# A three-layer float32 transformer on one core: unsplit value products in the first mixer, transposed retention queries, and another order of the first loads

## The chip, the cores and the metric

One core of a Trainium2 chip runs the whole program. The metric is the device time of one execution in microseconds (us), here the median of three. TensorE (PE) multiplies, ScalarE (ACT) and VectorE (DVE) work elementwise, GpSimd (POOL) does a few small things, SyncE (SP) issues most of the transfers.

## The reference

All is float32, one sequence of 256 tokens, width 1024. Two layers of a first block, each a mixer and a squared-ReLU MLP of width 4096, are followed by a hybrid layer with three attention branches and a final RMS norm. The change touches the two mixers:

```
def _window_gqa(q, k, v, sink):            # heads a: 8 query heads of 64, 2 key/value heads
...
    p = jnp.exp(s - m)
    p = p / (jnp.sum(p, axis=-1, keepdims=True) + jnp.exp(sk - m))
    o = jnp.einsum('bnhgqk,bnkhd->bqnhd', p.astype(v.dtype), vb)
...
def _even_mixer(x, norm_g, w_in, qn_a, kn_a, sink_a, qn_b, kn_b, rpb_b, w_out):     # first mixer
...
    qa, ka, va, qb, kb, vb = _split(h @ w_in, EVEN_SPLITS)
...
    return jnp.concatenate([oa, ob], axis=-1) @ w_out
...
def _odd_mixer(x, norm_g, w_in, dec_f, dec_b, gn_g, w_out):     # second mixer: retention, 8 heads
...
    q, k, v, g = _split(h @ w_in, ODD_SPLITS)
...
        a = jnp.einsum('bhid,bhjd->bhij', qc, kc) * dmask
        o = jnp.einsum('bhij,bhjv->bhiv', a, vc) + jnp.einsum('bhid,bhdv->bhiv', qc, R) * cross[:, :, None]
```

Heads b are neighbourhood attention, 8 heads of 64. Retention's queries and keys are 128 wide for each head, its values 256.

## The kernel before, in words

**Products.** Nearly every float32 product is made of three fast ones. A float32 operand is split into a high part (rounded to the type F32R, by ACT) and a low part (the difference, by DVE); `mm3` (L337 to L340) adds high by high, high by low and low by high. A few small products are unsplit: both operands stay F32, and PE takes the four-pass float32 path. In the rows such a product shows as two records.

**Panels.** A weight matrix comes in panels of 512 columns, 1024 rows, as two loads of 1 MB (tile `raw`, four buffers, `w_dma` L400). `w_hi` (ACT) and `w_lo` (DVE) turn each load into two pairs of tiles `whi` and `wlo`; for the MLP's input weights, once its pool is open, the pairs are called `mhi` and `mlo` and lie at another offset (`w_tile`, L440). `panel` (L495) keeps the activations stationary and moves 512 weight columns: 2 token tiles x 8 row tiles x 3 = 48 matmuls of 512 columns, result tokens by columns. `panel_T` (L542) keeps the weights stationary and moves 256 tokens: 4 x 8 x 3 = 96 matmuls of 256 columns, result columns by tokens. It serves the MLPs.

**Start.** `run` (L847) issues the first loads: the transposed input, the first panel in small pieces, then x (for the norm's statistics), constants, and the next two loads (the second panel, 256 columns wide, 512 KB each). `warm` (L883) gives PE small bf16 matmuls on zeros until the weights come. The first panel (`first_panel`, L516) makes the queries of heads a, the second their keys and values (ka, va), the third the queries of heads b (qb), then kb, vb, and two panels of another layer's memory keys and values (kx, vx).

**First mixer.** `qk_task` squares a panel's result on ACT (tile `qn`), reduces it on DVE, adds the norm's `em`, scales and transposes. The 16 heads go in pairs: `score_pair` (L723) makes both heads' scores, one on rows 0 to 63 and one on rows 64 to 127 of the array; `even_head` (L737) makes the softmax (tile `p`), four transposes on PE, splits the result into `ph` and `pl`, and multiplies by the split values (`vah`, `val`, `vbh`, `vbl`). Values are padded with zeros to 128 columns (`pads`, L992), so that two heads add into the two halves of one bank's rows, 6 matmuls of 256 columns for each.

**Second mixer.** `_odd` runs over four pairs of heads; for each pair one panel gives queries and keys (512 columns), one the values, one the gate. The query task (L1264) copies the panel's result to `nat`, and `split_T` (L673) transposes it four blocks at a time and splits it into `qkh` and `qkl`.

**Order.** The program is laid down by a planner of its own: generators yield conditions, `drive` (L157) keeps a model of when each engine, transfer and tile is free, and at each step takes the ready task with the best priority. Each engine executes its instructions in the order in which they were laid down. Constants of that model (rate of loads, start times such as `MEM`, `BIAS`, `DMA0`) move the order and nothing else.

Of the kernel before, what the change touches and what calls it, by code (L numbers as in the profile page):

```python
# [72 lines left out]
class Kernel:  # L73
# [17 lines left out]
    MEM, BIAS = 14.0, 16.0  # L91

    DMA0, FINE = 1.5, 4
# [299 lines left out]
    def load(self, eng, out, in_):  # L393

        eng.dma_start(out, in_)
        n = out.shape[0] * self._n(out) * 4
        self.free["D"] += max(n / 360e3, 0.18)
        self._mark(self.ready, out, self.free["D"] + 1.7, "D")

    def w_dma(self, a=None, b=4):  # L400
# [13 lines left out]
        else:  # L414
            self.nc.sync.dma_start(raw[:, :n], src)
            t0 = max(self.free["D"], self.rawfree[i - self.RAW] if i >= self.RAW else 0.0)
            self.free["D"] = t0 + P * n * 4 / 360e3
# [259 lines left out]
    def split_T(self, src, hi, lo, k0, t, key, scale=None):  # L677
# [8 lines left out]
        if k0 is None:  # L686
            pv = ps[:, :n * P].rearrange("p (a b q) -> p a b q", a=2, b=n // 2)
        else:
            pv = ps[:, :n * P].rearrange("p (i q) -> p i q", i=n)
            hi, lo = (v[:, k0:k0 + n, t * P:(t + 1) * P] for v in (hi, lo))  # L690
# [46 lines left out]
    def even_head(self, pool, ps, v, o, j, tab, init, sink=None):  # L737
# [25 lines left out]
        yield ("rdy", p)  # L763
        yield ("acq", "pT", 1)
        yield ("acq", "bank", 1)
# [10 lines left out]
        out = o[:, (j // 2 % 2) * S:(j // 2 % 2 + 1) * S]  # L776
        if j % 4:
            yield ("ev", ("pv", j - 1))
        yield ("op", "T", [], [ph, pl])
# [6 lines left out]
        self.fire(("pv", j), at=self.free["T"])  # L786
        self.give("pT")
        self.give("hd")
# [53 lines left out]
    def run(self):  # L842
# [24 lines left out]
        self.w_dma(0, 4)  # L867
        for t in range(NT):
            self.load(nc.sync, x[t], aps["x"][t * P:(t + 1) * P, :])
        self.load(nc.sync, const, aps["const"][:, :K_MAIN])  # L870
        for _ in range(self.RAW - 2):
            self.w_dma()
# [9 lines left out]
    def warm(self):  # L882
# [6 lines left out]
        yield 1.4  # L889
        while self.hcur < 3:  # L890
# [4 lines left out]
            self._pe(0.213 if self.now < 7 else 0.11, ps)  # L895
# [36 lines left out]
    def _even(self, pool):  # L932
# [899 lines left out]
```

## Time and profile before

| | |
|---|---|
| median of 3 runs | 996.02 us (996.0 to 997.14) |
| profiled execution, its own time | 997.11 us |
| its span, first to last instruction | 995.3 us |
| PE busy | 982.2 us, 99% of the span |
| DVE busy, ACT busy | 675.1 us (68%), 525.9 us (53%) |
| bytes read | 173.75 MB, 176 GB/s over the span |
| mean granted clock of PE | 0.997 |

The span is read from the first to the last instruction; the own time of the execution is 1.8 us longer. Busy shares are means over the whole span; what matters for an edit is which engine is waited for in its stage. Ends of matmuls are modelled, so that consecutive ones overlap in the rows: the distance between two starts is the price of one.

### The profile page before, as it was taken

The page shows a single profiled execution, that of the slowest core. Times are in us where ns is not written, and L with a number is a line of the kernel's source. Part 1 is how long each engine was busy: PE and PEld are TensorE (multiplying, and loading weights), DVE is VectorE, ACT ScalarE, POOL GpSimd, SP SyncE. Part 2 cuts the span into 40 slices and gives each one's busy share as a digit, 9 for nine tenths or more (in the row PEclk, how much of TensorE's full clock was granted, in tenths as well). Part 3 has the DMA queues.
Part 4 walks back from the last instruction along what each step waited for, and adds up shares of the span by engine and source line. Part 5 has one row for each costly group of instructions (what it writes and reads, how often), then busy time and mean ns, then how long its engine had stood idle before and what let it go on. Part 6 is the DMA issues. An engine that isn't in the chain of part 4 may idle for free.

```text
span 995.3 us, 14096 instructions
## 1 busy us (share of the span) xinstructions
PE 982.2 (99%) x5559; PEld 844.6 (85%) x5559; DVE 675.1 (68%) x1134; ACT 525.9 (53%) x821; POOL 30.4 (3%) x38
## 2 busy tenths in 40 slices
PE   8999999999999999999999999999999999999997
PEld 6787889999998888888889999998888888878885
DVE  6898567554457977877657555446779866677774
ACT  7777656433345655555446553334564554454453
POOL 1220000000000000000000000000100000000000
PEclk9999999999999999999999999999999999999999
DMA  9733455555445544443555555542544436544431
GB/s 351 285 133 122 134 175 205 218 209 202 170 169 175 184 166 163 167 168 138 194 187 171 209 209 214 212 171 97 203 157 141 156 139 205 192 173 148 180 127 42
DMA packets 27266, 175.71 MB, mean 177 GB/s; under 512 B 3200, under 2 KB 3584, under 8 KB 7616
## 3 DMA queue, kind: packets, MB, share of 16 engines
q1 hardware_dynamic: 25776, 171.49, 48.0%
q0 software_dynamic: 704, 2.49, 1.0%
q8 instruction: 43, 0.70, 0.3%
q10 hardware_dynamic: 720, 0.84, 0.3%
q14 instruction: 23, 0.19, 0.1%
HBM read 173.75 MB, written 1.05 MB: 176 GB/s over the span
## 4 chain that ended last, share of the span: by engine, by line
PE 97%; DVE 2%; ACT 0%; DMA 0%; issue 0%; POOL 0%; DVEq 0%; POOLq 0%
PE bank L332 93%; PE bank L343 4%; DVE p L279 1%; DMA tb<-in_xT 0%; DVE pl L257 0%; DVE p L265 0%; DVE st L289 0%; PE bank L894 0%; ACT ph L252 0%; ACT nraw L252 0%; ACT u L252 0%; DVE x L257 0%; DVE wlo L257 0%; ACT qn L252 0%; DVE o L257 0%
## 5 line engine op out<-in xcount | busy, mean ns | idle before, releaser
L257 DVE TENSOR_TENSOR wlo<-raw,whi 128x1024 fp32r<-128x1024 f32 (+2 forms) x266 | 311.5, 1183 | 89.6 <-ACT whi L252 87.9
L252 ACT ACTIVATE whi<-raw 128x1024 fp32r<-128x1024 f32 (+2 forms) x266 | 268.5, 1024 | 131.9 <-PE bank L332 131.3
L332 PE MATMUL bank<-whi,xh 128*128 128x512 f32 (+2 forms) x592 | 233.8, 397 | 2.2 <-ACT whi L252 2.2
L332 PE MATMUL bank<-wlo,xh 128*128 128x512 f32 (+2 forms) x592 | 227.5, 384 | 0.4 <-DVE wlo L257 0.4
L332 PE MATMUL bank<-whi,xl 128*128 128x512 f32 (+2 forms) x592 | 227.7, 385 | 0.0
L332 PEld LDWEIGHTS bank<-whi,xh 128*128 128x128 f32 x592 | 112.2, 190 | 23.0 <-ACT whi L252 3.1
L332 PEld LDWEIGHTS bank<-whi,xl 128*128 128x128 f32 x592 | 112.2, 190 | 22.2
L332 PEld LDWEIGHTS bank<-wlo,xh 128*128 128x128 f32 x592 | 112.5, 190 | 19.7 <-DVE wlo L257 0.6
L332 PE MATMUL bank<-xh,mlo 128*128 128x256 f32 x464 | 128.2, 276 | 0.0
L332 PE MATMUL bank<-xh,mhi 128*128 128x256 f32 x464 | 128.2, 276 | 0.0
L332 PE MATMUL bank<-xl,mhi 128*128 128x256 f32 x464 | 128.2, 276 | 0.0
L257 DVE TENSOR_TENSOR h<-h 128x512 f32<-128x512 f32 x32 | 22.0, 688 | 115.4 <-ACT h L252 115.4
L332 PE MATMUL bank<-whi,hh 128*128 128x512 f32 x256 | 100.2, 391 | 0.0
L332 PE MATMUL bank<-wlo,hh 128*128 128x512 f32 x256 | 99.8, 390 | 0.0
L332 PE MATMUL bank<-whi,hl 128*128 128x512 f32 x256 | 99.7, 389 | 0.0
L252 ACT ACTIVATE h<-bank 128x512 f32<-128x512 f32 x32 | 18.8, 588 | 137.4 <-PE bank L332 137.4
L332 PEld LDWEIGHTS bank<-xh,mhi 128*128 128x128 f32 x464 | 87.1, 188 | 0.5
L332 PEld LDWEIGHTS bank<-xl,mhi 128*128 128x128 f32 x464 | 87.1, 188 | 0.4
L332 PEld LDWEIGHTS bank<-xh,mlo 128*128 128x128 f32 x464 | 87.1, 188 | 0.0
L257 DVE TENSOR_TENSOR mlo<-raw,mhi 128x1024 fp32r<-128x1024 f32 x58 | 68.6, 1219 | 1.2 <-ACT mhi L252 1.2
L252 ACT ACTIVATE mhi<-raw 128x1024 fp32r<-128x1024 f32 x58 | 58.2, 1047 | 0.8 <-PE bank L332 0.8
L332 PEld LDWEIGHTS bank<-whi,hl 128*128 128x128 f32 x256 | 48.1, 188 | 10.2
(250 smaller groups left out, 1337.3 us busy)
## 6 DMA issues: line engine op xcount, KB each, us to landing
raw<-in_w_mlp_in SPq DMA_DIRECT2D x32, 1024.0 KB, 4.9
raw<-in_w_mlp_out SPq DMA_DIRECT2D x32, 1024.0 KB, 4.9
raw<-in_w_in SPq DMA_DIRECT2D x32, 1024.0 KB, 4.8
raw<-in_w_in_o SPq DMA_DIRECT2D x24, 1024.0 KB, 4.8
raw<-in_w_out_o SPq DMA_DIRECT2D x8, 1024.0 KB, 4.9
raw<-in_w_in_e SPq DMA_DIRECT2D x6, 1024.0 KB, 9.2
raw<-in_w_up SPq DMA_DIRECT2D x6, 1024.0 KB, 4.7
raw<-in_w_mem SPq DMA_DIRECT2D x4, 1024.0 KB, 4.9
```

The lines of the kernel that those rows point to most:

```text
L252: self.nc.scalar.activation(out, in_, func, scale=scale, **kw)
L257: self.nc.vector.tensor_tensor(out, a, b, op=op)
L279: self.nc.vector.tensor_tensor_reduce(out, a, b, scale, init, op0, op1, acc)
L332: self.nc.tensor.matmul(out, lhsT, rhs, start=start, stop=stop, skip_group_check=shared)
L343: self.nc.tensor.transpose(out, in_, self.ident)
```

## The change

- `run`: the two loads behind the first panel (in the loop over `RAW - 2`) are issued before x and the constants. Planner constants: `BIAS` 30 instead of 16, `DMA0` 2.3 instead of 1.5, loads at 405 instead of 360 GB/s, `distances` 28 instead of 20 us after the start.
- `warm`: 24 matmuls at once, then more only while the first weights are awaited.
- First mixer: values are copied unsplit (`va`, `vb`), no pads. `even_head` copies the transposed probabilities unsplit to `pT`; the second head of a pair waits for the first and then multiplies both: per half of the keys, one product for rows 0 to 63 of the bank and one for rows 64 to 127, 64 columns of values each.
- Second mixer: queries and keys come from `panel_T` and are split from the bank; for the first pair of heads the value panel goes first.

```
-        for t in range(NT):
-            self.load(nc.sync, x[t], aps["x"][t * P:(t + 1) * P, :])
-        self.load(nc.sync, const, aps["const"][:, :K_MAIN])
         for _ in range(self.RAW - 2):
             self.w_dma()
+        for t in range(NT):
+            self.load(nc.sync, x[t], aps["x"][t * P:(t + 1) * P, :])
+        self.load(nc.sync, const, aps["const"][:, :K_MAIN])
...
+        for _ in range(self.WARM):
+            self.nc.tensor.matmul(ps[:, :256], zero[:, :P], zero[:, :256], start=True, stop=True)
+            self._pe(0.213, ps)
...
-        ph, pl = (pool.tile([P, 512], F32R, name=n, tag=n, bufs=2) for n in ("ph", "pl"))
-        yield from self.split(ph, pl, ps)
+        tiles[j] = pool.tile([P, 512], F32, name="pT", tag="pT", bufs=4)
+        end = yield from self.act(tiles[j], ps, AF.Copy)
         self.done(ps)
+        self.give("hd")
+        if j % 2 == 0:
+            self.fire(("pTs", j), at=end)
+            return
+        yield ("ev", ("pTs", j - 1))
...
+        both = [(i, tiles.pop(i)) for i in (j - 1, j)]
+        yield ("op", "T", [], [b[1] for b in both])
+        cols = slice((j // 2 % 2) * S, (j // 2 % 2 + 1) * S)
         for kt in range(2):
-            vh, vl = v(kt)
             ks = slice(kt * S, (kt + 1) * S)
-            self.mm(out, vh, ph[:, ks], j % 2 == 0 and kt == 0, False)
-            self.mm(out, vl, ph[:, ks], False, False)
-            self.mm(out, vh, pl[:, ks], False, j % 2 == 1 and kt == 1)
+            for i, pT in both:
+                self.mm(o[64 * (i % 2):64 * (i % 2) + 64, cols], values(i, kt), pT[:, ks], kt == 0, kt == 1,
+                        beside=i == j)
...
-                    yield from self.split(vap(vdst[t][0], [[P, 2], [1, 64]]), vap(vdst[t][1], [[P, 2], [1, 64]]),
-                               vap(ps[:, P:], [[64, 2], [1, 64]]), self.r[t])
+                    yield from self.act(vdst[t], ps[:, P:2 * P], AF.Copy, scale=self.r[t])
...
-            for e in range(2):
-                hi, lo = (vap(v[:, e * P:], [[192, 4], [1, 64]]) for v in vb[t])
-                end = yield from self.split(hi, lo, vap(ps[:, e * 64:], [[P, 4], [1, 64]]), self.r[t])
+            end = yield from self.act(vb[t], ps, AF.Copy, scale=self.r[t])
...
-            def task(t, ps):
-                yield ("acq", "nat", 1)
-                nat = pool.tile([P, 512], F32, name="nat", tag="nat", bufs=2)
-                yield from self.act(nat, ps, AF.Copy)
-                self.done(ps)
-                yield from self.split_T(nat, *(vap(v[:, t * P:], [[KO, 2], [S, 2], [1, P]]) for v in qk), None, t,
-                                        ("rqk", hp, t))
-                self.give("nat")
+            def task(b, ps):
+                qs = slice(b * KO, b * KO + 2 * S)
+                end = yield from self.split(qk[0][:, qs], qk[1][:, qs], ps)
+                self.done(ps)
+                self.fire(("rqk", hp, b), at=end)
...
-            yield from self.panel(self.xT, "xo", qk_task(hp, qk), tmajor=hp == 0)
+            if hp == 0:
+                yield from self.panel(self.xT, "xo", v_task(hp, vv), tmajor=True)
+            yield from self.panel_T(self.xT, "xo", qk_task(hp, qk))
```

The new constants and the moved loads change the order of instructions. ACT at the end of the first panel, before the change (`xh` and `xl` are the input's parts, `whi` the weights' high part, `nraw` the squares of x for the statistics, `qn` the square of the first panel's result, `vah` to `vbl` the padded values):

```order
L252 ACTIVATE xh<-tb 128x256
L252 ACTIVATE whi<-raw 128x512
L252 ACTIVATE nraw,ss_112<-x_70 128x512 x2
L252 ACTIVATE nraw,ss_113<-x_71 128x512 x2
L252 ACTIVATE vah_121<-const 128x64
L252 ACTIVATE val_122<-const 128x64
L252 ACTIVATE vah_123<-const 128x64
L252 ACTIVATE qn<-bank 128x512
L252 ACTIVATE val_124<-const 128x64
L252 ACTIVATE qn<-bank 128x512
L252 ACTIVATE vbh_127<-const 128x4x64
L252 ACTIVATE whi<-raw 128x512 x2
```

The same place in the change:

```order
L252 ACTIVATE xh<-tb 128x256
L252 ACTIVATE whi<-raw 128x512 x3
L252 ACTIVATE nraw,ss_112<-x_70 128x512
L252 ACTIVATE whi<-raw 128x512
L252 ACTIVATE nraw,ss_112<-x_70 128x512
L252 ACTIVATE nraw,ss_113<-x_71 128x512 x2
L252 ACTIVATE qn<-bank 128x512 x2
L252 ACTIVATE whi<-raw 128x1024 x4
```

The last row of `whi` before the statistics was the first panel's; now all four pieces of the second panel stand ahead of `qn`, three of them ahead of the squares of x, and the pads are gone.

SP's queue, the change against before (- and + as usual; `tb<-in_rpb` is the table of heads b, `mem` the memory input):

```order
 L395 DMA raw<-in_w_in_e 128x512 x4
+L415 DMA raw<-in_w_in_e 128x1024 x2
 L395 DMA x_70<-in_x 128x1024
 L395 DMA x_71<-in_x 128x1024
 L395 DMA const<-in_const 128x640
-L415 DMA raw<-in_w_in_e 128x1024 x2
-L1003 DMA dist<-in_dist 128x384
+L1004 DMA dist<-in_dist 128x384
 L415 DMA raw<-in_w_in_e 128x2048 x2
-L1064 DMA mem<-in_mem 128x1024
-L948 DMA tb<-in_rpb 128x3072
```

The two 512 KB loads pass x and the constants; the table, which stood behind `mem`, goes behind four more 1 MB loads of weights.

PE at one pair of heads a, before the change (`kTa,qTa` are scores, `const,p` transposes):

```order
L332 MATMUL bank<-kTa,qTa 128x256 x4
L332 MATMUL bank<-ph,vah_121 128x256
L332 MATMUL bank<-ph,val_122 128x256
L332 MATMUL bank<-pl,vah_121 128x256
L332 MATMUL bank<-ph,vah_123 128x256
L332 MATMUL bank<-ph,val_124 128x256
L332 MATMUL bank<-pl,vah_123 128x256
L343 MATMUL bank<-const,p 128x128 x4
```

and in the change:

```order
L343 MATMUL bank<-const,p 128x128 x4
L332 MATMUL bank<-pT,va_121 64x256 x2
L332 MATMUL bank<-pT,va_122 64x256 x2
L332 MATMUL bank<-whi,xh 128x512
L332 MATMUL bank<-wlo,xh 128x512
L332 MATMUL bank<-whi,xl 128x512
L332 MATMUL bank<-kTa,qTa 128x256 x4
```

Six products for one head have become four for two heads, behind the second head's transposes.

## Rows read from the trace of the kernel before

**Rows 1.** The page's part 1: busy us, share of the span, instructions of each engine.

```profile
PE 982.2 (99%) x5559; PEld 844.6 (85%) x5559; DVE 675.1 (68%) x1134; ACT 525.9 (53%) x821; POOL 30.4 (3%) x38
```

**Rows 2.** PE's waits over the span: who waited for whom, us, times, longest.

```profile
PE bank L332 <- DVE pl L257: 1.4, 4, 0.6
PE bank L332 <- ACT ph L252: 1.3, 3, 0.7
```

**Rows 3.** Timeline of PE, second panel: start, us, operation, out<-in, [idle before <-releaser].

```profile
21.60 0.38 PE L332 MATMUL bank<-whi,xh 128*128 128x256 f32 x1 [1.69 <-ACT whi L252]
22.36 0.38 PE L332 MATMUL bank<-wlo,xh 128*128 128x256 f32 x1 [0.38 <-DVE wlo L257]
```

**Rows 4.** Timeline of ACT at the end of the first panel.

```profile
19.50 0.60 ACT L252 ACTIVATE qn<-bank 128x512 f32<-128x512 f32 x1 [1.97 <-PE bank L332]
```

**Rows 5.** Timeline of SP's queue; transfers issued from 8 to 13 us, us to landing.

```profile
10.65 1.02 SPq L415 DMA_DIRECT2D raw<-in_w_in_e  x2
...
12.65 3.12 SPq L415 DMA_DIRECT2D raw<-in_w_in_e  x2
...
DMA packets 819, 1.92 MB, mean 383 GB/s; under 512 B 89, under 2 KB 89, under 8 KB 819
...
raw<-in_w_in_e SPq DMA_DIRECT2D x2, 512.0 KB, 7.4
raw<-in_w_in_e SPq DMA_DIRECT2D x1, 1024.0 KB, 9.3
```

**Rows 6.** Busy us by stretch, then granted clock, DMA share, GB/s.

```profile
23.60:26.90 3.30, 3.30 (x18) 3.30 (x17) 2.63 (x6) 2.32 (x4) 2.29 (x2) 0.50 1.05 441
```

**Rows 7.** Timeline of DVE, statistics of the first panel's result.

```profile
20.13 1.32 DVE L289 TENSOR_REDUCE st<-qn 128x8 f32<-128x512 f32 x2 [2.42 <-ACT qn L252]
```

**Rows 8.** Timeline of PE: the first warm-up block, two matmuls of the first panel.

```profile
1.09 4.24 PE L894 MATMUL bank<-vx 128*128 128x256 bf16 x19 [1.09 <-DVE vx L885]
...
9.27 0.63 PE L332 MATMUL bank<-wlo,xh 128*128 128x512 f32 x1
9.70 0.53 PE L332 MATMUL bank<-whi,xl 128*128 128x512 f32 x1
```

**Rows 9.** Timeline of PE: first product of one head, and what follows its sixth.

```profile
56.56 0.38 PE L332 MATMUL bank<-ph,vah 128*128 128x256 f32 x1
...
57.38 0.38 PE L343 MATMUL bank<-const,p 128*128 128x128 f32 x2
```

**Rows 10.** Timeline of PE: one pair's scores.

```profile
43.96 1.13 PE L332 MATMUL bank<-kTa,qTa 64*128 64x256 f32 x8
```

**Rows 11.** Timeline of PE: unsplit products of the hybrid layer's cross attention.

```profile
729.80 2.75 PE L332 MATMUL bank<-kx,xqT 128*128 128x256 f32 x12
```

**Rows 12.** Instructions on tile pl: duration ns min/median/max, first and last start.

```profile
L257 DVE TENSOR_TENSOR pl<-bank,ph x16: 675/684/692, 47.9 to 105.7; 128x512 fp32r<-128x512 f32 x16
L332 PEld LDWEIGHTS bank<-pl,vah x16: 187/188/188, 48.7 to 72.0; 128*128 128x128 f32 x16
```

**Rows 13.** Timeline of PE: a run of 512-column matmuls and one group of retention's transposes.

```profile
324.46 0.39 PE L332 MATMUL bank<-whi,xh 128*128 128x512 f32 x1
...
329.22 0.60 PE L343 MATMUL bank<-const,nat 128*128 128x128 f32 x4
329.58 0.48 PE L332 MATMUL bank<-whi,xh 128*128 128x512 f32 x1
329.89 0.40 PE L332 MATMUL bank<-wlo,xh 128*128 128x512 f32 x1
```

**Rows 14.** Timeline of PE: ends of two runs of transposed panels in the MLP.

```profile
146.38 0.28 PE L332 MATMUL bank<-xh,whi 128*128 128x256 f32 x1
...
151.41 0.28 PE L332 MATMUL bank<-xh,mhi 128*128 128x256 f32 x1
...
159.75 0.28 PE L332 MATMUL bank<-xh,mhi 128*128 128x256 f32 x1
...
167.23 0.40 PE L332 MATMUL bank<-whi,hh 128*128 128x512 f32 x1
```

More of the change, by code (lines that the diff above doesn't have):

```diff
@@ L396, in load @@
         n = out.shape[0] * self._n(out) * 4
-        self.free["D"] += max(n / 360e3, 0.18)
+        self.free["D"] += max(n / 405e3, 0.18)
         self._mark(self.ready, out, self.free["D"] + 1.7, "D")
@@ L416, in w_dma @@
             t0 = max(self.free["D"], self.rawfree[i - self.RAW] if i >= self.RAW else 0.0)
-            self.free["D"] = t0 + P * n * 4 / 360e3
+            self.free["D"] = t0 + P * n * 4 / 405e3
             self._mark(self.ready, raw, self.free["D"] + 2.2, "D")
@@ L685, in split_T @@
             self.transpose(ps[:, i * P:(i + 1) * P], src[:, i * P:(i + 1) * P])
[L686 to L690, printed above, removed]
+        pv = ps[:, :n * P].rearrange("p (i q) -> p i q", i=n)
+        hi, lo = (v[:, k0:k0 + n, t * P:(t + 1) * P] for v in (hi, lo))
         end = yield from self.split(hi, lo, pv, scale)
@@ L735, in score_pair, with even_head @@
         return ps
-    def even_head(self, pool, ps, v, o, j, tab, init, sink=None):
+    def even_head(self, pool, ps, o, j, tab, init, tiles, values, sink=None):
         p = pool.tile([P, 512], F32, name="p", tag="p", bufs=self.hb)
@@ L763, in even_head @@
         yield ("rdy", p)
+        if j:
+            yield ("ev", ("pT", j - 1))
         yield ("acq", "pT", 1)
+        self.fire(("pT", j))
         yield ("acq", "bank", 1)
@@ L867, in run @@
         self.w_dma(0, 4)
+        for _ in range(self.RAW - 2):
+            self.w_dma()
         for t in range(NT):
@@ L894, in warm @@
             self.nc.tensor.matmul(ps[:, :256], zero[:, :P], zero[:, :256], start=True, stop=True)
-            self._pe(0.213 if self.now < 7 else 0.11, ps)
+            self._pe(0.11, ps)
         self.done(ps)
@@ L988, in _even @@
         kTa = pool.tile([P, 1, S], F32, name="kTa")
-        va = [[pool.half(256, F32R, name=f"va{n}{t}") for n in "hl"] for t in range(NT)]
-        def pads():
-            for v, n in [(v, 1) for t in range(NT) for v in va[t]] + [(v, 4) for t in range(NT) for v in vb[t]]:
-                yield from self.act(vap(v[:, 64:], [[192, n], [1, 64]]), vap(self.const[:, K_CM:], [[0, n], [1, 64]]), AF.Copy)
-        self.spawn(pads(), 12.0, self.LOW)
+        va = [pool.half(P, F32, name=f"va{t}") for t in range(NT)]
         qTb = pool.tile([P, 4, S], F32, name="qTb", tag="qTb")
         kTb = pool.tile([P, 4, S], F32, name="kTb")
-        vb = [[pool.half(768, F32R, name=f"vb{n}{t}") for n in "hl"] for t in range(NT)]
+        vb = [pool.tile([P, 512], F32, name=f"vb{t}") for t in range(NT)]
         oT = [[pool.tile([P, 4, S], F32R, name=f"o{n}0") for n in "hl"], []]
-        self.res["pT"], self.res["tab"] = 2, 2
+        self.res["pT"], self.res["tab"] = 4, 2
+        tiles = {}
         tabs = {}
@@ L1079, in _even, with values @@
         yield from self.panel(self.xT, "xe", qk_task("ka", 2, kTa, 1.0, va))
+        def values(j, kt):
+            v, h = (va, j % 2) if j < 8 else (vb, j - 8)
+            return v[kt][:, 64 * h:64 * h + 64]
         def head_a(j, o, ps):
-            h, n = A_ORDER[j], j % 2
-            vc = slice(64 * n, 64 * n + P)
+            h = A_ORDER[j]
             def tab():
@@ L1088, in tab @@
                 return tabs.pop(j)
-            return self.even_head(pool, ps, lambda kt: (va[kt][0][:, vc], va[kt][1][:, vc]), o, j, tab,
-                                  nsink[:, h:h + 1], cols[:, C_SINK + h:C_SINK + h + 1])
+            return self.even_head(pool, ps, o, j, tab, nsink[:, h:h + 1], tiles, values,
+                                  cols[:, C_SINK + h:C_SINK + h + 1])
         self.spawn(even_heads())
```

30 lines of the change are left out of this document (13 added, 17 removed).

## The prediction

> **What bounds the kernel now.** I read the page first: TensorE (PE) is busy for 982.2 of 995.3 us [rows 1], so the time is what PE has to do plus the few gaps in front of it. The list of PE's waits came next. Its long entries name tiles that exist only at the start: the weights of the second panel, and the probabilities ph and pl of the first mixer, 1.3 and 1.4 us [rows 2]. Outside these stages PE never waits for a tile. So an edit counts where it takes PE work away, adds some, or touches a wait in the first mixer. ACT and DVE work taken away elsewhere lies beside PE and is worth nothing.
>
> **The second panel (order of loads).** PE stands idle 1.69 us for ACT's whi, has one matmul at 21.60, and goes on at 22.36, when DVE's wlo is there [rows 3]. The reader is to see the cause in ACT's row before: ACT itself stood 1.97 us until 19.50 at the square of the first panel's result (qn), for which it needed the end of that panel [rows 4]. ACT takes its work in order, and whi stood behind qn. The transfer was not late: issued at 10.65, 7.4 us to landing, 18 [rows 5]. In the change both weight loads go ahead of x and const (1.37 MB, 3.6 us at 383 GB/s [rows 5], so they land near 14.5), and ACT converts all four pieces ahead of qn. The wait ends: 1.69, and 22.36 - 21.60 less that matmul's own 0.12, is 2.3 us. It has a second price. After the gap the granted clock is at half, 1.2 instead of 2.4 GHz, from 23.6 to 26.9 [rows 6]: 3.3 us at half speed lose 1.6 us. With no gap in front I expect no fall. Together **-3.9 us**.
>
> What becomes late instead is x, by two loads of 512 KB, 1.05 MB, 2.7 us. Its statistics are needed on DVE after the reduction of qn, which starts at 20.13, lasts 1.32 and had DVE idle for 2.42 before it [rows 7]: 3.7 us are free, and I cost it at nothing; without that cover the first heads would slip by the difference. The third panel needs the 1 MB load issued at 12.65, 9.3 us to landing [rows 5], 22; with one conversion on ACT and one on DVE (some 1.2 each) 24.4. PE would come to it at about 18.9 + 48 x 0.12 = 24.7. That is 0.3 us to spare, the weakest place of this sum. The table rpb goes behind four more loads of weights, some 11 us at the same rate, and is read only by the last eight heads; nothing.
>
> **The first panel.** 24 warm-up matmuls now stand in a row. 19 of them take 4.24 us from 1.09 [rows 8], so 24 end at 6.4, where now a real matmul, two fillers and another wait alternate; the second pair of real ones waits for its weights in both orders. In the panel matmuls start 0.43 us apart as late as 9.27 to 9.70 [rows 8], against 0.23 at full clock. With full spacing from 7.4 the other 46 matmuls and three fillers end at 7.4 + 46 x 0.227 + 0.3 = 18.1 plus any wait for weights, against 19.75 now; with half spacing until 12 they end 1 us later than now. An unbroken row of fillers speaks for the earlier end, the weights' arrival against a full gain. I take **-0.6 us**, ends -1.6 and +1.0.
>
> **The value products.** Now a head has 6 matmuls of 256 columns, 56.56 to 57.38 [rows 9]: 0.82, and 1.64 us for two heads. In the change a pair has 4 unsplit products of 64 output rows each, two at a time on the two halves of the columns. The trace has no such form. From one side: a score pair, 4 unsplit products of 256 columns, two at a time on the two halves of the rows, is 8 records in 1.13 us [rows 10]. From the other: unsplit products of 256 columns over the whole array run one behind the other, 12 records in 2.75 us with the last one's tail [rows 11], so some 1.7 for 8. I take the first, which differs only in the side of the array that is halved, with 0.1 for the change of form: 1.64 - 1.23 = 0.4 a pair, eight pairs, **-3.2 us**. Serial, 1.7 + 0.1 against 1.64 makes +0.15 a pair, +1.2.
>
> **The waits in the heads.** 2.7 us now [rows 2]. The change takes 16 subtractions of 0.684 us (pl, 47.9 to 105.7 us) off DVE [rows 12], and the values' splits; ACT keeps as many conversions. But the heads come some 4 us earlier against weights that arrive as now, and PE is sooner at each next one. I take half, **-1.4 us**; ends -2.7 (all gone) and +1.0 (new ones).
>
> **Retention.** Each of four panels (queries and keys of two heads) loses 2 groups of 4 transposes. A group takes 329.22 to 329.58, 0.36, and the matmul behind it 0.31 instead of 0.227 [rows 13]: 0.445, eight of them, -3.6 us. But the panel's form changes, from 48 matmuls of 512 columns to 96 of 256 with the weights stationary, and for this shape the trace has two prices. With weights in the tiles mhi and mlo, 66 take 159.75 to 167.23, 0.1133 each; with whi and wlo, as at the MLP's start, 42 take 146.38 to 151.41, 0.1198 each [rows 14]. Retention's weights are whi and wlo. So 96 x 0.1198 = 11.50 stands against 48 x 0.2267 = 10.88 (21 from 324.46 to 329.22 [rows 13]): +0.62 a panel, +2.5 us. Net **-1.1 us**; by the first price it would be -3.6. ACT's copies (nat), the value panel put first for the first two heads and the planner's new constants cost or bring nothing, since PE waits for nothing there.
>
> **Sum.** -3.9 - 0.6 - 3.2 - 1.4 - 1.1 = -10.2 us. The profiled execution took 997.1 (the span and 1.8 around it), 1.1 above the median of 996.02. From it this gives 986.9, from the median 985.8; I say **986.0**.
>
> **Rivals.** (1) The column halves do not overlap: 1.2 more instead of 3.2 less, 4.4 us of gain gone, **990.5**. For it: only halves of the rows are seen to overlap here. (2) Slower than before: the halves' weight loads are not hidden either. A load of 128 columns takes 0.188 us [rows 12]; ahead of each of 8 records this is 1.7 + 8 x 0.188 = 3.2, 1.6 more than now, +12.6 us over the eight pairs, and with the other terms (-7.0) **1001.6**. It decides from 0.9 us above today's pair, 2.5 us. Against it: the score pairs' eight loads cost nothing that shows. The Trainium skill ("TensorE: Matmul & The Clock Gate", Part 3: Packing small matmuls) says that a weight load overlaps a running matmul only where the row group differs; two halves of the columns share theirs, so by that rule (2) would hold. The same part gives 2.38 times for three column tiles, which speaks for the forecast. No run so far shows either. (3) The start gives part back: the third panel's weights come after PE, a gap of 1 us opens near 24.7, the clock falls once more (1.6), and the heads keep their waits (1.4): 4 us of gain gone, **990**. For it: 0.3 us of slack. (4) The edit does not act: x's lateness stops the heads for what the weights gain, the halves are serial, retention's two terms cancel: within 2 us of **996**.
>
> **How the numbers follow.** Forecast 0.62, (1) 0.18, (2) 0.04, (3) 0.13, (4) 0.03. The low end is the forecast with all waits gone and the first panel at its best (-2.3, 983.7) and half of the better price in retention (-1.2): 982.5. The high end takes in (1) and (3) with 1 us of their own spread: 991.5. Left out are (2), (4), and (1) with (3). 0.2% is 2 us, about what a measurement can tell from no change. Faster: forecast, (1) and (3), 0.93; same: (4), 0.03; slower: (2), 0.04.
>
> **What would show it.** Right: no wait of PE for whi or wlo near 20 us, a granted clock of 1.00 through 20 to 30; the 64-row products in blocks of about 1.1 us for 8 records; retention's 256-column matmuls 0.12 apart; no waits for pl. Wrong: blocks of 1.7 us or more, a gap before the third panel, a longer list of waits in the heads.

## The result, and the profile after

The changed kernel takes 984.47 us, median of 4 runs (984.15 to 985.23), where the kernel before took 996.01 on the same chip: a ratio of 0.9883, 95% interval 0.9866 to 0.99. That is 11.5 us less by the medians. The profiled execution's span fell from 995.3 to 982.6, 12.7 us; before's profiled execution lay 1.1 above its median, which is most of the difference between the two figures.

The first part of the page, to be held against [rows 1]:

```profile
PE 974.0 (99%) x5687; PEld 841.1 (86%) x5687; DVE 664.5 (68%) x1112; ACT 519.0 (53%) x803; POOL 30.3 (3%) x38
```

PE is busy for 8.2 us less, so some 4.5 of the 12.7 us are idle time that went and the rest is busy time, what was lost at half clock included. PE's waits, to be held against [rows 2] (tile waited for, engine, us in total, times, longest):

```profile
PE bank L332 <- ACT whi L252: 0.5, 1, 0.5
PE bank L343 <- DVE den L257: 0.2, 1, 0.2
```

The probabilities have left the list altogether, and of the waits for weights only the one in the first panel is left. Timeline of PE from the warm-ups to the third panel (start, us, operation, out<-in, [idle before <-releaser]), to be held against [rows 3] and [rows 8]:

```profile
1.09 5.28 PE L894 MATMUL bank<-vx 128*128 128x256 bf16 x24 [1.09 <-DVE vx L888]
6.04 0.80 PE L332 MATMUL bank<-whi,xh 128*128 128x512 f32 x2
7.38 0.73 PE L332 MATMUL bank<-whi,xh 128*128 128x512 f32 x2 [0.54 <-ACT whi L252]
...
18.17 0.39 PE L332 MATMUL bank<-whi,xl 128*128 128x512 f32 x1
18.40 0.28 PE L332 MATMUL bank<-whi,xh 128*128 128x256 f32 x1
...
24.03 0.28 PE L332 MATMUL bank<-whi,xl 128*128 128x256 f32 x1
24.15 0.39 PE L332 MATMUL bank<-whi,xh 128*128 128x512 f32 x1
```

The reader is to see three joints without a gap: the first real matmul behind the 24 warm-ups, the second panel at 18.40 right behind the last matmul of the first, and the third at 24.15. Windows of the second panel and the start of the third (busy us of PE, PEld, DVE, ACT and POOL, then the granted clock), to be held against [rows 6]:

```profile
19.00:22.00 3.00, 3.00 (x28) 3.00 (x27) 2.23 (x8) 2.00 (x7) 1.61 (x3) 1.00 1.03 429
22.00:25.00 3.00, 3.00 (x24) 2.85 (x23) 2.25 (x4) 2.28 (x3) 3.00 (x2) 1.00 1.00 418
```

The clock stays at 1.00 where it was 0.50 before. Timeline of ACT in the same place, to be held against [rows 4]:

```profile
17.48 0.62 ACT L252 ACTIVATE whi<-raw 128x512 fp32r<-128x512 f32 x1
...
19.23 0.61 ACT L252 ACTIVATE nraw<-x 128x512 f32<-128x512 f32 x1
...
19.84 1.06 ACT L252 ACTIVATE qn<-bank 128x512 f32<-128x512 f32 x2
21.90 1.06 ACT L252 ACTIVATE whi<-raw 128x1024 fp32r<-128x1024 f32 x1 [1.00 <-DMA raw<-in_w_in_e]
```

The second panel's last conversion is done before qn begins. So are the squares of x (nraw), and they hold qn: it begins at 19.84, 0.34 later than before, although the first panel ends 1.35 earlier. The third panel's first conversion waits a whole microsecond for its load. PE starts that panel at 24.15 and its first product with DVE's low part at 24.38; DVE had made that part by some 24.2. Timeline of PE at one pair's value products, to be held against [rows 9]:

```profile
56.86 1.08 PE L332 MATMUL bank<-pT,va 128*64 128x256 f32 x8
57.88 0.55 PE L343 MATMUL bank<-const,p 128*128 128x128 f32 x3
```

Eight records from 56.86 to the next instruction at 57.88: 1.02 us for two heads. Retention's panel of queries and keys, and the first matmul on mhi in each of the two MLPs, which I use as marks of the stages:

```profile
139.85 0.28 PE L332 MATMUL bank<-xh,mhi 128*128 128x256 f32 x1
...
324.04 0.28 PE L332 MATMUL bank<-xl,whi 128*128 128x256 f32 x1
324.16 0.28 PE L332 MATMUL bank<-xh,wlo 128*128 128x256 f32 x1
...
515.87 0.28 PE L332 MATMUL bank<-xh,mhi 128*128 128x256 f32 x1
```

Timeline of PE in the kernel before: the last matmul of the first panel, the first of the third, and the second MLP's mark (the first MLP's, 151.41, is in [rows 14]):

```profile
19.52 0.39 PE L332 MATMUL bank<-whi,xl 128*128 128x512 f32 x1
...
30.45 0.40 PE L332 MATMUL bank<-whi,xh 128*128 128x512 f32 x1
...
528.81 0.28 PE L332 MATMUL bank<-xh,mhi 128*128 128x256 f32 x1
```

So the start and the first mixer gave 11.56 us, the stretch from the first MLP through retention to the second MLP 1.38 (377.40 to 376.02), and the rest of the program took 0.24 back (466.49 to 466.73); this last is not the change's own, since in e2 below, where PE has the same instructions in the same order from there on, it is 466.4 again.

### The profile page after: what moved, and what is told of

It is laid out like the page before. It is cut to its first block, busy times and chain, and to the rows that moved or that the text cites. A ratio compares the mean times of both kernels' runs of the same rounds, so it can differ in the third digit from the quotient of the medians.

```text
span 982.6 us, 14333 instructions
## 1 busy us (share of the span) xinstructions
PE 974.0 (99%) x5687; PEld 841.1 (86%) x5687; DVE 664.5 (68%) x1112; ACT 519.0 (53%) x803; POOL 30.3 (3%) x38
## 4 chain that ended last, share of the span: by engine, by line
PE 95%; DMA 3%; ACT 1%; DVE 0%; issue 0%; POOLq 0%; SPq 0%; ACTq 0%
PE bank L332 91%; PE bank L343 4%; DMA raw<-in_w_in_e 2%; DMA mem<-in_mem 1%; DMA tb<-in_xT 0%; ACT whi L252 0%; ACT nraw L252 0%; DVE wlo L257 0%; ACT u L252 0%; DVE x L257 0%; DVE qn L257 0%; POOLq L1821 0%; ACT qTa L252 0%; DVE xl L273 0%; SPq L395 0%
## 5 line engine op out<-in xcount | busy, mean ns | idle before, releaser
L332 PE MATMUL bank<-whi,xh 128*128 128x512 f32 (+2 forms) x528 | 206.9, 394 | 0.5 <-ACT whi L252 0.5
L332 PE MATMUL bank<-whi,xl 128*128 128x512 f32 (+2 forms) x528 | 201.6, 382 | 0.0
L332 PE MATMUL bank<-wlo,xh 128*128 128x512 f32 (+2 forms) x528 | 201.3, 381 | 0.0
L332 PEld LDWEIGHTS bank<-whi,xh 128*128 128x128 f32 x528 | 99.2, 188 | 20.1 <-issue 2.5
L332 PEld LDWEIGHTS bank<-whi,xl 128*128 128x128 f32 x528 | 99.2, 188 | 19.5
L332 PEld LDWEIGHTS bank<-wlo,xh 128*128 128x128 f32 x528 | 99.5, 188 | 16.4
```

The costliest lines, as they stand in the source:

```text
L332: self.nc.tensor.matmul(out, lhsT, rhs, start=start, stop=stop, skip_group_check=shared)
```

## The experiments

All were timed in three rounds beside the kernel before. They are edits of the changed kernel, whose 984.47 us and span of 982.6 are what "more" and "less" refer to. They ran in three groups on three chips; the kernel before took 995.97 to 996.21 us beside them and 996.01 beside the change, so a few tenths of a microsecond between them tell nothing.

### Do the two halves of the columns overlap?

**e1: the products of one half in a row, then those of the other.**

```
-        for kt in range(2):
-            ks = slice(kt * S, (kt + 1) * S)
-            for i, pT in both:
+        for i, pT in both:
+            for kt in range(2):
+                ks = slice(kt * S, (kt + 1) * S)
```

> The changed kernel, with the four value products of a pair in another order: both products of the first head's half of the columns, then both of the second's, instead of alternating. Same work, same tiles. Theory (products on different halves overlap, products on the same half don't): only one of the seven joints between the 8 records overlaps as before, so a block of 8 records grows from 1.02 us to about 1.5 us (7 x 0.213), eight blocks cost 3 to 4 us, 987.5 to 988.5 us. Rival (no overlap; a product of 64 output rows is simply cheap): the blocks stay at 1.0 to 1.1 us and the time at 984.5.

Measured: 984.48 us, nothing changed; the blocks still last 1.02. I took it, by the numbers on record, as evidence against any overlap, and went on with the reading that a half-size record is cheap by itself. That was wrong, as the next run shows.

**e9: one head's products once more.** The two products of the pair's first head are done twice, into the same place.

```
+        for kt in range(2):
+            self.mm(o[:64, cols], values(both[0][0], kt), both[0][1][:, kt * S:(kt + 1) * S], kt == 0, kt == 1)
         for kt in range(2):
             ks = slice(kt * S, (kt + 1) * S)
             for i, pT in both:
```

> The changed kernel, with the value products of the first head of each pair (4 records, 64 output rows) done once more ahead of the four products of the pair, into the same place; the output stays. Theory now held, after the products of one half in a row cost no more: a record of a 64-row product costs 0.13 us by itself, whatever stands beside it. Then a block of 12 records takes 1.02 + 4 x 0.128 = 1.53 us and the eight pairs cost 4.1 us more: 988.6 us. Rival A, the theory of the forecast: a record costs as much as one over the whole array, 0.2267, and is cheap only in company of one on the other half; then the four records without company cost 0.91, the block 1.93 and the run 7.3 us more: 991.8. Rival B: PE would have waited for the probabilities or the scores there, and the added records lie in that time: below 986.

Measured: 989.55 us, 5.1 more. The time lies between the theories; the blocks decide. The first row is a block of e9 in the timeline of PE, up to the instruction behind it:

```profile
56.25 1.94 PE L332 MATMUL bank<-pT,va 128*64 128x256 f32 x12
58.12 0.55 PE L343 MATMUL bank<-const,p 128*128 128x128 f32 x3
```

From 56.25 to 58.12 is 1.87: four more records on the same half cost 0.85, 0.21 each, and not 0.13. So a half-size record alone costs what a full one costs, and it is the company that makes the block cheap: rival A's price. How e1 could still be as fast is seen when the timeline is cut short inside a block, so that a row counts only the records that had begun by then. In e1, up to 56.94 and up to 57.14:

```profile
56.82 0.44 PE L332 MATMUL bank<-pT,va 128*64 128x256 f32 x2
...
56.82 0.66 PE L332 MATMUL bank<-pT,va 128*64 128x256 f32 x4
```

In e9, up to 51.70 and 51.86:

```profile
51.34 0.65 PE L332 MATMUL bank<-pT,va 128*64 128x256 f32 x2
...
51.34 0.92 PE L332 MATMUL bank<-pT,va 128*64 128x256 f32 x4
```

In e1, where the program has two products of the first half ahead of the first of the second, two records have begun within 0.12 us all the same, and they go on in twos. In e9, where three products of the first half stand ahead of the first one of the second, the block begins with single records 0.2 apart and doubles up only about 0.5 us later. The rows do not name the half of a record, but the counts do: in this block of e9 eight records start 0.22 apart (51.34, 51.61, 51.82, 52.04, 52.25, 52.47, 52.68, 52.90) and four more between them (51.83, 52.09, 52.31, 52.53), as many as the two heads have. The two halves therefore run as two streams beside each other, and PE looked past two products of one half (e1) to start the other half's. That PE executes in the order in which instructions were laid down, as the description of the kernel has it, does not hold across the halves. A block lasts about as long as its longer half: 8 records of 0.21 and a start of some 0.17 in e9, 4 of them and the same start in the changed kernel. Over the whole mixer the blocks of e9 sum to 14.8 us against 8.6, 6.2 more, and the stage's end came 5.4 later; where the other 0.8 went I did not find.

**e10: the same question for the rows.** The forecast took its price from the score pair, two products on the two halves of the rows.

```
-        for both in ops:
-            for i, (a, b, q, k) in enumerate(both):
-                self.mm(ps[i][:, a:b], q, k, True, True, beside=i == 1)
+        for i in range(2):
+            for both in ops:
+                a, b, q, k = both[i]
+                self.mm(ps[i][:, a:b], q, k, True, True, beside=i == 1)
```

> The changed kernel, with the products of a score pair in turn (both of the first head, on one half of the rows, then both of the second) instead of alternating. The forecast priced the value products by the score pair, as two products that run beside each other on the two halves. Theory: as with the value products the order does not matter, a half-size record costs about 0.13 by itself; blocks of 8 records stay at 1.06 to 1.13 us, and the time at 984.5. Rival A: on the halves of the rows there is overlap, and alternation is what gives it; in turn 8 records take 8 x 0.2267 = 1.8 us, 0.7 more for each of eight pairs of the first mixer, 5.6 us, and up to as much again in the last stage: 990 to 996. Rival B: partial, the two products of one head next to each other lose only where the head changes; blocks of 1.3 to 1.5, 987 to 988.

Measured: 984.73 us, no change that can be measured. In the timeline of PE one block of eight in full, and one cut at 37.44:

```profile
37.33 0.49 PE L332 MATMUL bank<-kTa,qTa 64*128 64x256 f32 x2
...
43.18 1.14 PE L332 MATMUL bank<-kTa,qTa 64*128 64x256 f32 x8
```

Two records have begun within 0.11 us, though the program has two of one head first. The number is the theory's, but not for its reason: the halves of the rows are two streams in the same way. The two products of one head write different columns here and still go 0.22 apart, so it is the half that makes the stream, not the place that is written.

### What the unsplit products are worth, and the waits

**e12: values and probabilities split again,** the rest as changed. The edit puts `even_head`, the value tiles, their pads and the values' splits back as they stand in the listing of the kernel before.

> The changed kernel with values and probabilities split again, as in the kernel before (six products of a head, the subtractions pl on DVE, the values in two tiles with pads); order of loads, warm-ups and retention stay changed. Theory, by the stage's own length in the two traces (6.1 us shorter): 990.6 us, with waits for ph and pl back in the list. The forecast's own sizes (3.2 for the products, 1.4 for waits): 989.1. Rival A: products alone by their blocks (1.64 against 1.06, eight pairs, 4.6) and waits twice that of the kernel before, since the heads now come 5 us earlier against the same DVE: 993 or more. Rival B: the pads on ACT ahead of the second panel's weights return and open the gap again, +2 on top of the theory, with a wait for whi near 19 us.

Measured: 990.89 us, 6.4 more; the span is 6.5 longer and the first matmul on mhi comes 6.8 later (146.64). PE's waits:

```profile
PE bank L332 <- DVE pl L257: 1.6, 4, 0.6
...
PE bank L332 <- ACT whi L252: 0.9, 1, 0.9
PE bank L332 <- ACT ph L252: 0.6, 2, 0.3
```

This is the theory's 990.6. The waits for pl and ph are 2.2 us and no more than before (2.7 in [rows 2]), though the heads come some 5 us earlier, so rival A falls; the second panel followed the first without a gap (18.25 to 18.48), so rival B falls too. Of the 6.8 us the blocks of value products account for 6.7: adding up, over the timeline, the time from the first product of a block to the next instruction that is none gives 15.3 us here and 8.6 in the changed kernel.

**e6: the DVE load put back alone.** Each head gets a subtraction of 128x512 that nobody reads, as `pl` was.

```
+        spare = pool.tile([P, 512], F32, name="spare", tag="spare", bufs=2)
+        self.nc.vector.tensor_tensor(spare, ps, tiles[j], op=ALU.subtract)
```

> The changed kernel with the 16 subtractions of 128x512 (0.684 us each on DVE) put back behind each head's copy of the transposed probabilities; their result is not used. Theory (the heads' waits of 2.7 us went because DVE is relieved of 10.9 us): PE's waits for p or den come back, 1 to 2.5 us slower, 985.5 to 987. Rival (they went because no product waits for DVE's low part any more, whatever DVE has to do): under 0.5 us, 984.5 to 985.

Measured: 989.28 us, 4.8 more, and the first matmul on mhi 5.1 later: more than I had expected. The waits of PE that are new:

```profile
PE bank L343 <- DVE p L265: 1.2, 3, 0.4
PE bank L343 <- DVE den L257: 1.2, 1, 1.2
```

PE now waits for the softmax itself: 16 subtractions of 0.684 us [rows 12] are 10.9 us of DVE work, and nearly half of it reaches PE. The list shows 2.4 us of the 5.1. The rest is not in the order of the heads, since but for the subtractions PE, ACT and DVE execute the changed kernel's instructions in the changed kernel's order; whether it is in joints too short to be listed was not taken apart. What it does show is that in this stage DVE work is not free beside PE; the prediction had called it free only elsewhere. It is no price for these subtractions in general: the edit does not enter them into the planner's model, so nothing was laid down around them, and each one also reads the bank of the transposes, which is free only behind it. In e12 the planner knew of the same 16 subtractions, and PE's waits there were 2.2 us.

### The start

**e2: x and the constants first again.**

```
-        for _ in range(self.RAW - 2):
-            self.w_dma()
         for t in range(NT):
             self.load(nc.sync, x[t], aps["x"][t * P:(t + 1) * P, :])
         self.load(nc.sync, const, aps["const"][:, :K_MAIN])
+        for _ in range(self.RAW - 2):
+            self.w_dma()
```

> The changed kernel, with x and the constants loaded ahead of the second panel's weights again, and so with ACT's square of the first panel's result (qn) again ahead of those weights. Theory (place in ACT's queue, gap, half clock): PE idle about 2 us ahead of the second panel, granted clock at half for about 3 us behind it, 3.5 to 4.5 us slower than the change, 988 to 989. Rival A (only the gap counts, the clock would have fallen anyway or does not fall): 2.3 us slower, 986.8. Rival B (x's earlier arrival gives back what the weights lose): 984.5.

Measured: 986.17 us, 1.7 more. Timeline of ACT and of PE between the panels, and a window of the second:

```profile
18.41 0.60 ACT L252 ACTIVATE qn<-bank 128x512 f32<-128x512 f32 x1 [1.73 <-PE bank L332]
18.90 1.14 ACT L252 ACTIVATE whi<-raw 128x512 fp32r<-128x512 f32 x2
```

```profile
18.43 0.39 PE L332 MATMUL bank<-whi,xl 128*128 128x512 f32 x1
19.57 0.38 PE L332 MATMUL bank<-whi,xh 128*128 128x256 f32 x1 [0.75 <-ACT whi L252]
20.37 0.39 PE L332 MATMUL bank<-wlo,xh 128*128 128x256 f32 x1 [0.42 <-DVE wlo L257]
```

```profile
20.00:21.00 1.00, 0.63 (x5) 0.63 (x6) 1.00 (x4) 1.00 (x4) 0.00 (x0) 1.00 1.03 434
```

The gap is back, with qn ahead of whi on ACT as in [rows 4], but it is 1.6 us (18.66 to 19.57, and 19.69 to 20.37), since neither the pads nor a second qn stand ahead of whi any more. Counted in the same way the gap of the kernel before is 2.5 (19.75 to 21.60, and 21.72 to 22.36); the prediction's 2.3 took the idle time as the rows print it. The granted clock stayed at 1.00 behind the gap, and its mean is 0.999 in all four executions. The first matmul on mhi comes at 141.98, 2.1 later: the gap, a first panel that ends 0.26 later, and two waits for p, 0.6 in all, which the changed kernel does not have, come to some tenths more than that. So the order of loads alone, in this company, is worth 1.7 us by the medians, and the half clock of the kernel before belongs to its longer gap or to something else.

**e11: a longer gap.** To e2, two copies on ACT ahead of the second panel's first conversion.

```
+            for _ in range(2 if n == 4 else 0):
+                self.nc.scalar.activation(self.vx[0], self.xTraw[:, 8:520], AF.Copy)
             for i, c in enumerate(self.w_parts(n)):
                 yield from self.act(hi[:, c], raw[:, c], AF.Copy)
```

> The order of loads of the kernel before (x and const ahead of the second panel's weights, as in e2_x_first, 986.17 us, where PE stood some 1.6 us ahead of the second panel and the granted clock stayed at 1.00), and two copies of 128x512 on ACT that nobody reads, right ahead of the conversion of the second panel's first weights: some 1.05 us more of gap, 2.6 in all, where the kernel before had 2.3 and half clock behind it. Theory: the gap alone brings the half clock; the records show 0.50 for some 3 us of the second panel, which costs 1.6 beside the 1.05: 988.8 us. Rival A: the half clock of the kernel before came from something else than the length of the gap; the clock stays at 1.00 and only the 1.05 us counts: 987.2. Rival B: neither counts, because the first heads wait for the statistics of x and not for the panel: 986.2.

Measured: 986.06 us, as e2. It tested nothing: the copies were laid down earlier than meant, in time in which ACT was free, as its timeline shows:

```profile
13.41 1.28 ACT L449 ACTIVATE vx<-tb 128x512 f32<-128x512 f32 x2
```

PE's gap was 1.6 us again, the clock 1.00 again. The second panel's first conversion began at 18.84, as in e2. Whether the longer gap alone would have brought the half clock stays open.

**e5: 19 warm-ups, and idle time until the first weights are there.**

```
-    DMA0, WARM, FINE = 2.3, 24, 4
+    DMA0, WARM, FINE = 2.3, 19, 4
...
+        yield ("if", lambda: self.hcur >= 1)
```

> The changed kernel with 19 instead of 24 warm-up matmuls in a row, and no further filler until the second tile of weights is in use, so that PE stands idle for about 0.6 us ahead of the first real matmul, as it did before the change. Theory (the unbroken row brings the full clock earlier, and that is what ended the first panel 1.35 us earlier): matmuls of the first panel 0.43 us apart for some 2 us longer, 0.7 to 1.4 us slower, 985.2 to 985.9. Rival (the weights' arrival and the place of the fillers among the real matmuls decide): 984.5 and the first panel ends at 18.4.

Measured: 984.78 us, 0.3 more, which is within what can be told from nothing; the profiled span is 1.1 longer. Timeline of PE and a window behind it:

```profile
6.01 0.73 PE L332 MATMUL bank<-whi,xh 128*128 128x512 f32 x2 [1.28 <-ACT whi L252]
7.66 1.22 PE L332 MATMUL bank<-whi,xh 128*128 128x512 f32 x2 [0.92 <-ACT whi L252]
8.68 0.63 PE L332 MATMUL bank<-wlo,xh 128*128 128x512 f32 x1
9.11 0.63 PE L332 MATMUL bank<-whi,xl 128*128 128x512 f32 x1
```

```profile
8.00:10.00 2.00, 2.00 (x6) 1.48 (x5) 2.00 (x5) 1.49 (x5) 0.00 (x0) 0.50 1.02 390
```

After idle stretches of 1.28 and 0.92 us the clock is at half and the matmuls 0.43 apart, as they were before [rows 8]. (The windows of the kernel before print 1.00 there; their clock records begin at 9.96, and the spacing tells.) The second panel starts at 20.08 instead of 18.40, 0.3 of it because the second pair waits longer for its weights. In this execution, then, the idle stretches cost the first panel its clock; no trace with the 24 warm-ups shows half clock from the second pair on. But this was the slowest of four executions, with a mean clock of 0.996. The other three have 0.998, as the changed kernel has, and two of them its span of 982.6, so that the loss need not come every time. In the median the unbroken row's worth, 0.3 us, can't be told from nothing.

### Retention, and where its tiles lie

**e3: queries and keys as before,** 48 matmuls of 512 columns and the transposes of `nat`; the value panel stays first.

```
-            yield from self.panel_T(self.xT, "xo", qk_task(hp, qk))
+            yield from self.panel(self.xT, "xo", qk_task(hp, qk))
```

> The changed kernel, with retention's queries and keys made as before (48 matmuls of 512 columns and 8 transposes a pair of heads), the value panel still first for the first pair. Theory (96 matmuls at 0.1198 us against transposes of 0.445 a group): 1.1 to 1.4 us slower than the change, 985.6 to 985.9. Rival (the transposed panel runs at the MLP's 0.1133): 3.6 us slower, 988. Second rival (transposes were hidden, only the panel's price counts): 2.5 us faster, 982.

Measured: 985.99 us, 1.5 more; span 1.1 more. Timeline of PE, the first matmul on mhi in each of the two MLPs:

```profile
139.54 0.28 PE L332 MATMUL bank<-xh,mhi 128*128 128x256 f32 x1
...
516.94 0.28 PE L332 MATMUL bank<-xh,mhi 128*128 128x256 f32 x1
```

The start is 0.31 shorter here, and the stretch between the marks is 377.40 again, just as before the change. So all of the 1.38 belongs to queries and keys, and the value panel put first is worth nothing that shows. The forecast's 1.1 holds in cause and is 0.3 too low; the price of the tiles mhi and mlo (3.6) falls, and so does a gain of nothing.

**e4: the MLP's weight tiles without their offset of 64 bytes.** The two prices of one shape, 0.1133 and 0.1198 [rows 14], had no stated cause.

```
-            return halfway(self.mpool, 1024, F32R, name="m" + part, tag="m" + part, bufs=self.WB)
+            return self.mpool.tile([P, 1024], F32R, name="m" + part, tag="m" + part, bufs=self.WB)
```

> The changed kernel, with the MLP's weight tiles mhi and mlo laid at the start of their tile, as whi and wlo are, instead of 16 elements (64 bytes) into it; nothing else moves. Theory (the 64-byte offset of the stationary operand makes 0.1133 instead of 0.1198 us): the 464 x 3 matmuls of this form go to 0.1198 each, 9 us slower, 993.5. Rival (the two prices come from something else, such as the stage or what ACT and DVE write meanwhile): they stay at 0.1133 and the time at 984.5.

Measured: 993.49 us, 9.0 more, as expected. The groups by line, of the changed kernel (first) and of e4 (busy us, mean ns):

```profile
L332 PE MATMUL bank<-xh,mhi 128*128 128x256 f32 x464 | 128.2, 276 | 0.0
```

```profile
L332 PE MATMUL bank<-xh,mhi 128*128 128x256 f32 x464 | 131.2, 283 | 0.0
```

1392 matmuls in three such groups become 6.5 ns dearer each, and that alone is 9.0 us. So where the tiles mhi and mlo lie decides between the two prices. Whether it is their own address or its distance from another operand's is not shown.

**e7: the same offset for all other weights' high parts.** `whi` 64 bytes in, as mhi; the pool grows by 640 bytes and moves the pools behind it.

```
+        if part == "hi":
+            return halfway(self.wp, 1024, F32R, name="w" + part, tag="w" + part, bufs=self.WB)
```

> The changed kernel with all whi tiles 64 bytes into their tile, wlo tiles left at its start. Theory (the stationary operand's offset sets 0.1133 or 0.1198, each matmul by its own tile; a moving operand of 512 columns doesn't care): in retention's transposed panels the two matmuls of three with whi go to 0.113, the one with wlo stays; 4 x 64 x 0.0065 = 1.7 us there and 0.6 at the starts of the MLPs, 982.2. Rival A (moving operands do care, in the other direction): the 512-column matmuls on whi get dearer, 0.2267 to more, and the time rises above 984.5. Rival B (both tiles must be offset): no gain, 984.5.

Measured: 996.12 us, 11.6 more, the whole gain gone. **e8: a pad of 64 bytes ahead of that pool,** which moves it and every later one by 64.

```
+        self.wp.tile([P, 16], F32, name="shift")
```

> The changed kernel with 64 bytes put ahead of the pool of the weights, so that raw, whi and wlo all lie 64 bytes further. Theory (as for the run before, by the stationary operand alone): all 384 transposed matmuls of retention and the 96 or more at the starts of the MLPs at 0.1133, 2.5 + 0.6 to 0.9 us faster, 981 to 981.5, a version better than both. Rival (moving operands or ACT and DVE pay for it): 512-column matmuls above 0.2267, or whi and wlo above 1.05 and 1.22 us, and a time of 984.5 or more.

Measured: 990.86 us, 6.4 more. Groups by line, of the changed kernel, of e7 and of e8 in this order (mean ns of one behind the busy time):

```profile
L332 PE MATMUL bank<-xh,whi 128*128 128x256 f32 x176 | 50.6, 287 | 0.0
L332 PE MATMUL bank<-whi,hh 128*128 128x512 f32 x256 | 100.2, 391 | 0.0
```

```profile
L332 PE MATMUL bank<-xh,whi 128*128 128x256 f32 x176 | 50.3, 286 | 0.0
...
L332 PE MATMUL bank<-whi,hh 128*128 128x512 f32 x256 | 101.4, 396 | 0.0
```

```profile
L333 PE MATMUL bank<-xh,whi 128*128 128x256 f32 x176 | 49.6, 282 | 0.0
L333 PE MATMUL bank<-xh,mhi 128*128 128x256 f32 x464 | 130.6, 281 | 0.0
```

In e8 the weights whi, now 64 bytes off, are 5 ns cheaper, as mhi was in [rows 14]; but mhi has lost its place and pays 5 ns on 1392 matmuls, some 7 us. The 512-column matmuls with hh stay at 391 in e8. In e7 they became dearer, where whi is the moving operand and hh lies elsewhere. And whi as the stationary tile, 64 bytes in, stayed nearly at its old price there (287 to 286), where e7's theory had put it at mhi's: 64 bytes into the tile is not the whole rule. No version that beats the changed kernel came out of this. In both runs something else moved that lost more; a version that shifts these tiles and holds all others in place was not tried.

## Why the prediction was right, step by step

The forecast held: 986.0 was predicted, 984.47 measured, within the range, and by its mechanism. Its terms against the two traces, whose spans differ by 12.7:

| term | predicted | read from the traces |
|---|---|---|
| second panel | -3.9 | -4.1 |
| first panel | -0.6 | -1.35 |
| value products | -3.2 | -3.5 |
| waits in the heads | -1.4 | -2.65 |
| retention | -1.1 | -1.4 |
| rest of the program | 0 | +0.2 |

- **Second panel.** It ends at 24.15 instead of 30.45, 6.30 earlier. Of that 1.35 is the first panel's, and 0.9 are two groups of transposes that stood in it before and now come later. Both parts of the term went as told, gap (2.5 us from start to start) and half clock (1.6). Whether the gap brought the half clock is less sure than the prediction had it: e2 shows a gap of 1.6 us without a fall of the clock. Nor does the fall come every time: of the thirty executions of the kernel before that were timed beside the experiments, three have a mean clock of 0.999, which 3.3 us at half alone would bring down to 0.998, and they took 0.5 to 1.4 us less than the medians of their rounds.
- **First panel.** Its end moved from 19.75 to 18.40. The matmuls keep full spacing from 7.38 on, so the best end of the bound (-1.6) was nearer than the middle that I took. e5 has the cause in its one trace, but not in its median, so it is not shown that each execution gains this.
- **Value products.** The size is right, though both numbers it came from were too high. The thirteen stretches of products before sum to 14.7 us, of which 2.65 are waits; the other 12.1 are 1.51 a pair and not 1.64, because six of the sixteen heads take 0.69 each and not 0.82. After, the eight blocks sum to 8.6, 1.08 each and not 1.23: the 0.1 added for the change of form was not there. Pricing column halves by the score pair's row halves was right, as e9 and e10 show: both are pairs of streams beside each other. Rival (1), a serial block of 1.7, did not happen. Nor did rival (2): eight weight loads and eight records fit into 1.02 us, where it needed over 2.5 to decide. The rule of the Trainium skill that stood beside it ("TensorE: Matmul & The Clock Gate", Part 3: Packing small matmuls) does not hold for the two halves of the columns here. A gain from column tiles, as the same part reports one, is there: 1.02 us for eight records, where one stream of eight takes 1.87 in e9. The rows had spoken against rival (2) from the start: PEld is busy for 844.6 us beside PE's 982.2 in a span of 995.3 [rows 1], most of it for matmuls on all rows of the array.
- **Waits in the heads.** This is the term that was mis-sized. I took half of 2.7 us, because I expected PE to run into other waits as soon as it came earlier. All of it went: the blocks hold 2.65 us of waits before and none is listed after but 0.2 for den. e12 brings 2.2 back, and e6 shows why nothing took their place: with the 16 subtractions gone from DVE the softmax is in time, and with them back, outside the plan, PE waits for it. The low end of the range had this case.
- **Retention.** Right in sign, size and cause: the panel's matmuls are 0.12 apart with weights in whi and wlo, e3 gives the whole 1.38 back, and e4 shows that the lower price that I set aside belongs to the place of the MLP's tiles.
- **What I costed at nothing.** x's lateness cost PE nothing, but not by the room that I had counted on DVE: ACT's squares of x end at 19.9 and hold qn itself, which began at 18.41 in e2, until 19.84. No wait of PE comes of it; qn's transposes now stand behind the second panel. The third panel's weights, which I called the weakest place: no gap, and 0.2 us of margin, since the first conversion waited 1.00 us for the load. Rival (3) missed by a few tenths. In e12, where pads stand in ACT's way, that conversion begins at 22.32 instead of 21.90, and the one wait for whi, 0.9 us, is still the first panel's.

## What to carry to other kernels

Two products that each fill half of the array are worth placing together and in equal number: the block lasts as long as the longer half, and their order matters little. When the producer that PE waits for is taken away, look in the rows for the next one that would be late; where none shows, the whole wait can go, as it did here. After any edit that moves a pool, look at the mean duration of untouched matmul groups first: 64 bytes decided over more time here than any single term of this change.

## What the runs showed of the hardware that I had not expected

- The same 256-column matmul costs 0.1133 or 0.1198 us by the place of its tiles; 64 bytes for the MLP's weights are worth 9.0 us (e4). Setting whi 64 bytes in, which also moves later pools by 640, cost 11.6 (e7), and moving the weights' pool and all later ones by 64 cost 6.4 (e8). The rule behind the three was not found.
- Matmuls on one half of the array don't hold up those on the other even where two products of one half stand first (e1, e10: two records begun within 0.12 us), while four more on one half cost 0.21 us each (e9).
- A gap of 1.6 us between panels (e2, twice with e11) left the granted clock at 1.00, 2.4 GHz; idle stretches of 1.28 and 0.92 us at the start (e5) were followed by 0.50, and so was the gap of 2.5 us in the kernel before. One idle stretch of 1.2 us behind the 24 warm-ups (e8) was not. What sets the difference was not found.
